# Attention scores in an encoder trunk: each head's high query rows over its low rows in one block of 128 rows, two products a head in place of three; order and places listed anew

## The chip, the cores and the metric

One Trainium2 chip, one of its cores. The metric is the device time of one execution in microseconds (us), the median of several runs. The core has five engines with a queue each: TensorE (PE, with PEld for its weight loads), VectorE (DVE), ScalarE (ACT), GpSimd (POOL) and SyncE (SP, which here issues DMA transfers). An engine works its queue off in order and waits where an instruction needs another engine's result.

## The reference

A trunk of two layers on an input `x` of 256 tokens by 1024 values, all in 32-bit floats. Each layer is a feed-forward block, a mixer and another feed-forward block, each followed by a layer norm. The mixer of layer 0 is a bidirectional mLSTM, that of layer 1 attention over a window of 128 tokens:

```python
for l in range(DEPTH):                       # 2
    x = layer_norm(ALPHA * x + 0.5 * swiglu(x, ffn_w_in[l, 0], ffn_w_out[l, 0]), ...)
    y = mlstm_mixer(x, ...) if l % 2 == 0 else window_attention(x, ...)
    x = layer_norm(ALPHA * x + y, ...)
    x = layer_norm(ALPHA * x + 0.5 * swiglu(x, ffn_w_in[l, 1], ffn_w_out[l, 1]), ...)
# window_attention: 16 query heads, 4 key/value heads, 64 values a head
p = x @ w_in                                 # q, k, v
s = q . k * HEAD_DIM ** -0.5 - slope * |t - s|        # masked where |t - s| > 128
m = max(max(s), sink);  pe = exp(s - m)
attn = pe / (sum(pe) + exp(sink - m))
y = (attn . v) @ w_out
```

## The kernel before

There are six stages, one behind the other: feed-forward, mLSTM, feed-forward, feed-forward, attention, feed-forward. Tokens are worked in two tiles of 128 (`t`).

**Precise products.** TensorE multiplies in a format that rounds its operands, so every operand is split in two: ACT copies it into the rounded format (`_hi`) and DVE subtracts that from the original (`_lo`). `mm3` then sums three products into one bank: hi by hi, hi by lo, lo by hi. Each weight piece of 128 x 1024 is loaded by DMA into a raw buffer (`w_raw`, `s_raw`), split into `w_hi` (ACT) and `w_lo` (DVE), and used by PE. The split buffers are a ring of ten. The feed-forward stages save products by a scheme with sums of weight blocks, some of them made by accumulating DMAs that POOL issues.

**Attention.** `proj` makes k, v and half of q; `k_turn` and `q_turn` transpose k and q on PE and split them into `kk` (hi, lo) and `q2`. k is written twice into the rows it is transposed from, so in `kk` rows 0 to 63 and rows 64 to 127 hold the same key head. `q_rest` makes the other half of q already transposed, in four parts spread over the first steps. A step `j` of eight handles two heads `a` = 0, 1. `scores(j)` multiplies, and one DVE instruction (in the profile CUSTOM_DVE_ANT_0 with a READ_ACCUMULATOR, in the order ISA) adds the distance term and leaves the row extreme in `nm`; ACT takes the exponential and sums it; POOL divides (`scale`); PE transposes (`turn`, products with `ident`), ACT and DVE split the result (`pr_hir`, `pr_lor`); `values` multiplies with v; ACT and DVE gather `o`, which is split into `q2`'s old place of that step; `out_proj` multiplies it with `at_w_out`. `q_rest` and `out_proj` are fitted in between. Before, the hi rows of both heads of a step stood in `q2[:, j, 0]` (head a on rows 64a to 64a + 63) and the lo rows in `q2[:, j, 1]`, and a product had 64 rows of contraction.

**What sets the order.** Nothing is issued as the Python code runs: `Program` records every operation, and `issue` plays them in the order that the table of numbers `ORDER` gives (differences of the recorded indices). `SLOTS` gives each tile's place in its ring, one character per use. So every instruction in the profile carries the line of `Engine`'s `issue` call (L317 before, L276 after), and has to be told by its tiles: `p` is a bank of TensorE's results, `q2r` is `q2`, `sc` the scores.

Of the kernel before, what the change touches and what calls it, by code (L numbers as in the profile page):

```python
# [39 lines left out]
    "0 10 -9 8 2 -9 11 -10 11 15 1 -26 11 1 -11 12 1 -12 13 12 -24 13 1 11 -10 1 1 1 1 1 8 -7 17 -37 28 10 1 72 "  # L40
    "-71 -15 104 -103 15 -10 134 -136 13 140 -139 -11 17 -5 100 -114 15 46 -58 17 -16 17 -16 1 17 24 117 -142 -6 "
    "19 -18 112 -105 131 -137 11 19 -12 1 4 -3 4 1 -4 5 -19 1 19 122 -140 13 -10 32 -34 48 -45 1 157 -156 13 36 "
    "-48 21 -6 47 -40 -6 148 -147 32 14 -40 1 42 -10 -38 1 10 -9 30 46 -45 6 1 9 -8 60 -67 8 -7 1 10 38 99 -140 "
    "-31 161 -71 -95 49 100 -93 -26 13 1 34 -72 199 -160 -27 32 -4 60 -59 26 -25 -41 -6 56 -46 1 1 38 -43 89 -39 "
    "-49 43 1 -43 97 -53 110 -105 39 -38 1 3 -44 52 -10 1 77 -41 66 -100 -51 86 -85 116 -52 30 -29 1 -15 -50 66 "
    "-63 48 107 -106 42 -41 72 -55 1 -66 62 18 1 -14 -4 19 47 -65 4 1 1 13 -30 18 19 57 -56 55 -49 1 1 4 45 -56 "
    "8 11 -7 1 -4 5 -13 19 52 -70 55 -19 20 147 -146 -44 -12 18 1 -18 58 -39 213 -212 69 -33 157 -178 26 77 -132 "
    "38 76 -84 141 -115 -50 9 4 86 -73 31 -32 26 -37 38 -19 15 -33 43 -29 30 1 -7 -107 119 -49 45 17 -16 -8 9 53 "
    "-99 47 -34 36 2 -13 -37 16 57 -3 -9 30 -82 40 -39 41 1 1 21 100 -110 -10 1 10 -9 36 -10 11 -22 132 -141 32 "
    "-81 86 122 -146 34 -14 91 -110 -10 11 -76 66 81 -52 14 -32 1 1 92 -75 -29 32 49 -48 -44 26 -11 12 45 -44 88 "  # L50
    "38 -125 -17 258 -240 97 -82 1 27 -67 57 17 -33 -16 26 -25 149 -133 10 1 -10 15 -4 -6 -4 15 9 -13 20 -6 -20 "
    "21 1 -11 52 -51 1 152 -100 1 70 -69 -44 50 -32 -17 40 -37 -26 46 45 -78 24 -23 13 1 -22 93 -70 45 -44 239 "
    "-222 -16 78 -66 24 33 -52 44 -17 58 -89 1 23 -53 54 216 -253 61 -17 34 55 -88 1 16 -15 16 109 -171 273 -268 "
    "3 243 -150 -95 57 27 130 -156 14 157 -167 -21 3 41 -40 1 1 16 -15 40 -15 -9 23 -45 23 16 8 1 37 -124 102 "
    "-27 13 -25 9 -32 49 14 178 -191 47 -61 189 -201 9 207 -185 -1 2 8 -25 26 1 1 -61 65 -14 1 -24 64 -30 -37 83 "
    "-55 1 -23 35 -3 -29 30 24 11 -31 41 -27 -15 12 4 -14 58 -47 -10 1 18 -34 73 -56 1 12 -11 7 9 20 -10 120 104 "
    "-238 7 161 -160 1 71 103 -173 21 -20 187 -173 -13 84 -81 -14 -68 83 -18 63 74 -92 -26 9 20 -19 17 -16 1 52 "
    "-63 51 -37 15 -14 -14 43 -42 -31 59 1 63 -78 1 -14 15 229 -228 113 -100 198 -210 13 12 147 -165 7 -13 190 "
    "-147 3 -15 -6 1 -12 13 -12 43 -30 1 3 168 -184 1 1 1 55 -41 16 -15 111 -86 -24 1 126 -102 70 -93 278 -265 "
    "-6 130 -109 -45 41 70 -69 98 -97 3 -14 12 48 153 -227 29 1 1 103 -125 23 -49 215 -161 -24 -3 113 -85 -23 28 "  # L60
    "1 -37 -6 38 6 90 -95 -24 30 1 -6 84 -77 1 1 1 1 -10 11 6 78 -77 1 92 -27 -64 3 1 -12 9 123 -119 71 -44 14 "
    "-44 33 99 -121 23 -22 78 -59 221 -220 -28 31 -22 -8 262 -261 117 -87 72 -94 3 1 21 94 -114 44 -43 44 -27 62 "
    "-34 -27 10 -8 26 69 -84 228 -258 46 1 -46 23 80 -100 -10 1 33 -26 18 34 -51 119 -52 -45 -20 21 7 -4 94 -34 "
# [1423 lines left out]
```

## Time and profile before

| what | value |
| --- | --- |
| median of 3 runs | 915.05 us (914.67 to 915.2) |
| the profiled execution: span from its first to its last instruction | 914.29 us |
| the profiled execution's own time | given by its span alone |
| instructions | 12376 |
| granted TensorE clock | 0.998 of full speed |
| DMA | 208.52 MB, mean 228 GB/s |
| attention stage | about 645 to 731 us |
| score products on PE | 670.0 to 709.9 us |

Of the rows that follow: `busy` is the time in which an engine worked on such an instruction; products overlap on PE, so their pace is read from the distance of their starts. `[0.68 <-ACT o L317]` behind a row is idle time of the engine ahead of it and what ended it. A row `670.83:711.44 ...` gives busy time with the count of instructions for PE, PEld, DVE, ACT and POOL in that stretch, then the granted clock, the DMA share and GB/s.

### The profile page before, as it was taken

To read this page: it belongs to the slowest core of one execution; us is meant where nothing else is said; L and a number is where in the kernel's file an instruction comes from. 1 tells how busy PE (TensorE), PEld (TensorE's weight loads), DVE (VectorE), ACT (ScalarE), POOL (GpSimd) and SP (SyncE) were. 2 spreads that over 40 slices of the span, in tenths; PEclk is the share of its full clock that TensorE was granted. 3 is DMA by queue.
4 is the path that set the end of the run, shared out by engine and by line. 5 is a ranking of instruction groups with operands and counts; after the bars stand their busy time and mean duration, and the time that the engine had idled before them with its cause. 6 is when DMAs were issued, how large, how long until landed. Compare 5 with 4: busy or idle time off the path is not lost.

```text
span 914.3 us, 12376 instructions
## 1 busy us (share of the span) xinstructions
PE 903.8 (99%) x4382; PEld 748.2 (82%) x4382; DVE 812.8 (89%) x987; ACT 576.8 (63%) x796; POOL 156.8 (17%) x200
## 2 busy tenths in 40 slices
PE   9999999999999999999999999999999999999996
PEld 7888888889988888887888888888887788888885
DVE  6998989997798999888999988899899899988897
ACT  6667567557655677565747666666488557666560
POOL 0211112113311121111012111120435311202110
PEclk9999999999999999999999999999999999999999
DMA  9999889558273889898957899987543396997971
GB/s 334 299 298 298 246 248 240 180 179 263 94 260 114 270 252 256 269 280 197 341 196 188 229 277 296 277 178 259 173 173 116 116 277 166 257 303 174 321 182 46
DMA packets 100670, 208.52 MB, mean 228 GB/s; under 512 B 6872, under 2 KB 21232, under 8 KB 100608
## 3 DMA queue, kind: packets, MB, share of 16 engines
q1 hardware_dynamic: 82832, 173.83, 54.1%
q0 software_dynamic: 17632, 33.64, 22.4%
q8 instruction: 34, 0.56, 0.2%
q10 hardware_dynamic: 144, 0.26, 0.1%
q14 instruction: 28, 0.23, 0.1%
HBM read 206.65 MB, written 1.05 MB: 227 GB/s over the span
## 4 chain that ended last, share of the span: by engine, by line
PE 96%; DMA 2%; DVE 1%; issue 1%; ACT 0%; DVEq 0%; POOL 0%; POOLq 0%
PE p L317 96%; DMA s_raw<-in_ffn_w_in_dram 1%; DMA ln_g<-in_ln_g_dram 1%; DVE w_lo L317 0%; DVE x L317 0%; ACT w_hi L317 0%; DVE h_lor L317 0%; DVEq L1483 0%; DVE hc_lor L317 0%; DVE t L317 0%; ACT xT_hi L317 0%; DVE stats L317 0%; DVE mv L317 0%; POOL ji L317 0%; DVE ident L317 0%
## 5 line engine op out<-in xcount | busy, mean ns | idle before, releaser
L317 ACT CAST w_hi<-s_raw 128x1024 fp32r<-128x1024 f32 x239 | 244.5, 1051 | 94.5 <-PE p L317 56.4
L317 DVE TENSOR_TENSOR w_lo<-s_raw,w_hi 128x1024 fp32r<-128x1024 f32 x239 | 285.6, 1218 | 19.6 <-ACT w_hi L317 15.6
L317 ACT CAST w_hi<-w_raw 128x1024 fp32r<-128x1024 f32 (+1 forms) x167 | 172.1, 1041 | 77.9 <-PE p L317 37.6
L317 DVE TENSOR_TENSOR w_lo<-w_raw,w_hi 128x1024 fp32r<-128x1024 f32 (+1 forms) x167 | 199.8, 1208 | 14.5 <-ACT w_hi L317 13.3
L317 PE MATMUL p<-w_hi,xT_hi 128*128 128x512 f32 x512 | 191.9, 394 | 0.8 <-ACT w_hi L317 0.5
L317 PE MATMUL p<-w_lo,xT_hi 128*128 128x512 f32 x512 | 192.1, 394 | 0.0
L317 PE MATMUL p<-w_hi,xT_lo 128*128 128x512 f32 x512 | 191.3, 394 | 0.0
L317 PE MATMUL p<-w_hi,h_lor 128*128 128x512 f32 (+1 forms) x323 | 119.9, 390 | 0.1
L317 PE MATMUL p<-w_hi,h_hir 128*128 128x512 f32 (+1 forms) x323 | 119.5, 391 | 0.0
L317 PE MATMUL p<-w_lo,h_hir 128*128 128x512 f32 (+1 forms) x323 | 118.6, 389 | 0.0
L317 PEld LDWEIGHTS p<-w_hi,xT_hi 128*128 128x128 f32 x512 | 95.8, 188 | 20.4 <-ACT w_hi L317 1.0
L317 PEld LDWEIGHTS p<-w_lo,xT_hi 128*128 128x128 f32 x512 | 96.0, 188 | 19.5 <-DVE w_lo L317 0.4
L317 PEld LDWEIGHTS p<-w_hi,xT_lo 128*128 128x128 f32 x512 | 96.1, 188 | 19.3 <-DVE xT_lo L317 0.3
L317 POOL DMA_DIRECT2D s_raw<-in_ffn_w_in_dram x43 | 52.2, 1266 | 329.0 <-DVE w_lo L317 90.5
L317 PE MATMUL p<-w_hi,S_hir 128*128 128x512 f32 x256 | 96.9, 390 | 0.0
L317 PE MATMUL p<-w_hi,S_lor 128*128 128x512 f32 x256 | 96.8, 390 | 0.0
L317 PE MATMUL p<-w_lo,S_hir 128*128 128x512 f32 x256 | 96.8, 390 | 0.0
L317 PEld LDWEIGHTS p<-w_hi,h_lor 128*128 128x128 f32 x323 | 60.6, 188 | 12.6 <-DVE h_lor L317 0.5
L317 PEld LDWEIGHTS p<-w_lo,h_hir 128*128 128x128 f32 x323 | 60.7, 188 | 12.2
L317 PEld LDWEIGHTS p<-w_hi,h_hir 128*128 128x128 f32 x323 | 60.5, 188 | 12.3 <-ACT h_hir L317 0.2
L317 PEld LDWEIGHTS p<-w_hi,S_hir 128*128 128x128 f32 x256 | 48.0, 188 | 10.5 <-ACT t L317 0.4
L317 PEld LDWEIGHTS p<-w_lo,S_hir 128*128 128x128 f32 x256 | 48.1, 188 | 10.1 <-DVE w_lo L317 0.2
(187 smaller groups left out, 1176.7 us busy)
## 6 DMA issues: line engine op xcount, KB each, us to landing
s_raw<-in_ffn_w_in_dram SPq DMA_DIRECT2D x101, 512.0 KB, 6.0
w_raw<-in_ffn_w_in_dram SPq DMA_DIRECT2D x58, 512.0 KB, 6.3
s_raw<-in_ffn_w_out_dram SPq DMA_DIRECT2D x55, 512.0 KB, 5.8
s_raw<-in_ffn_w_in_dram POOLq DMA_DIRECT2D x43, 512.0 KB, 7.1
w_raw<-in_ffn_w_out_dram SPq DMA_DIRECT2D x33, 512.0 KB, 7.1
w_raw<-in_ml_w_in_dram SPq DMA_DIRECT2D x24, 512.0 KB, 5.2
w_raw<-in_ffn_w_in_dram POOLq DMA_DIRECT2D x21, 512.0 KB, 7.8
s_raw<-in_ffn_w_in_dram SPq DMA_DIRECT2D x20, 256.0 KB, 6.1
```

What stands on the lines that cost most here:

```text
L317: f(*args, **kw)
```

## The change

Each head's 64 hi rows are put on partitions 0 to 63 and its 64 lo rows on 64 to 127 of one block `q2[:, j, a]`. Since both halves of `kk` hold the same keys, one product of 128 rows with `kk` hi gives q_hi k_hi + q_lo k_hi, and one with `kk` lo gives q_hi k_lo + q_lo k_lo. A head and token tile so takes two products of 128 rows instead of three of 64, and the sum has the lo by lo term besides. The evacuations of q into `q2` are done once for each head half, on 64 partitions each. ORDER and SLOTS are new lists from end to end.

```diff
 ORDER = (
-    "0 10 -9 8 2 -9 11 -10 11 15 1 -26 11 1 -11 12 1 -12 13 12 -24 13 1 11 -10 1 1 1 1 1 8 -7 17 -37 28 10 1 72 "
...
 SLOTS = {
-    "raw.0": ("210375894260ab315798a1b2380476593806142893750a61b4735a0286b12a940280"),
+    "raw.0": ("0143256891a2b0734568b203751469a87519234867ab051923a7b509812475630984"),
...
@@ q_turn
                 for j in range(4):
                     nc.tensor.transpose(p[:, j], qd[t][:, j], ident)
-                split_evac((q2[:, 0:4, 0, tok(t)], q2[:, 0:4, 1, tok(t)]), p)
+                for a in range(2):
+                    split_evac((q2[0:64, 0:4, a, tok(t)], q2[64:128, 0:4, a, tok(t)]), p[64 * a:64 * a + 64])
@@ q_rest
                         j = 4 + 2 * g + f
-                        split_evac((q2[:, j, 0], q2[:, j, 1]), p, qs_col[:, j - 4:j - 3])
+                        for a in range(2):
+                            r = slice(64 * a, 64 * a + 64)
+                            split_evac((q2[0:64, j, a], q2[64:128, j, a]), p[r], qs_col[r, j - 4:j - 3])
@@ scores
                 for t in range(2):
-                    for n_, (qe, ke) in enumerate(((0, 0), (0, 1), (1, 0))):
-                        for a in range(2):
-                            r = slice(64 * a, 64 * a + 64)
-                            nc.tensor.matmul(ps[a][:, t], q2[r, j, qe, tok(t)], kk[ke][r, g], start=n_ == 0, stop=n_ == 2)
+                    for a in range(2):
+                        for e in range(2):
+                            nc.tensor.matmul(ps[a][:, t], q2[:, j, a, tok(t)], kk[e][:, g], start=e == 0, stop=e == 1)
```

The numbers of instructions change by 32 products fewer on PE (64 score products for 96) and six split pairs more (six instructions each on ACT and DVE); the rest is the same work in another order.

PE at the scores of step 2. Before:

```order
L317 MATMUL p4_92<-xT_lo_137,w_hi8_76 128x256
L317 MATMUL p2_90<-kk_hir_4_0_227,q2r_4_0_238 128x256
L317 MATMUL p2_90<-kk_lor_4_0_228,q2r_4_0_238 128x256
L317 MATMUL p5_93<-kk_hir_4_0_227,q2r_4_0_238 128x256
L317 MATMUL p2_90<-kk_hir_4_0_227,q2r_4_0_238 128x256
L317 MATMUL p5_93<-kk_lor_4_0_228,q2r_4_0_238 128x256
L317 MATMUL p5_93<-kk_hir_4_0_227,q2r_4_0_238 128x256
L317 MATMUL p0_88<-ident_144,sc_4_5_234 128x128
```

The same place on PE after (`p5` and `p4` are the banks of heads 0 and 1):

```order
L276 MATMUL p3_91<-xT_hi_136,w_lo3_81 128x256
L276 MATMUL p6_94<-ident_144,sc_4_5_234 128x128
L276 MATMUL p5_93<-kk_hir_4_0_227,q2r_4_0_238 128x256
L276 MATMUL p5_93<-kk_lor_4_0_228,q2r_4_0_238 128x256
L276 MATMUL p4_92<-kk_hir_4_0_227,q2r_4_0_238 128x256
L276 MATMUL p4_92<-kk_lor_4_0_228,q2r_4_0_238 128x256
L276 MATMUL p6_94<-ident_144,sc_4_5_234 128x128
```

Six products of one token tile, the heads in turn, have become four, hi and lo keys in turn. In both programs the 16 groups stand in 18 unbroken runs.

DVE ahead of and in the first score step. Before:

```order
L317 TENSOR_TENSOR w_lo_78<-w_raw_67,w_hi_70 128x1024
L317 TENSOR_TENSOR kk_lor_0_228<-p_94,kk_hir_0_227 128x4x128
L317 TENSOR_TENSOR sc_1_230<-p_90,qs_row_0_225 128x512
L317 TENSOR_TENSOR w_lo_87<-w_raw_66,w_hi_72 128x1024
L317 ISA sc_5_234,nm_2_243<-p_89,dist_0_235,neg_sink 128x256
L317 ISA nm_2_243 128x1
L317 ISA sc_5_234,nm_2_243<-p_95,dist_0_235,neg_sink 128x256
L317 ISA nm_2_243 128x1
L317 TENSOR_TENSOR q2r_0_238<-p_90,q2r_0_238 128x4x128
L317 TENSOR_TENSOR w_lo_82<-w_raw_64,w_hi_69 128x1024
L317 ISA sc_1_230,nm_2_243<-p_89,dist_0_235,neg_sink 128x256
```

The same place on DVE after:

```order
L276 TENSOR_TENSOR sc_2_231<-p_95,qs_row_0_225 128x512
L276 TENSOR_TENSOR kk_lor_0_228<-p_91,kk_hir_0_227 128x4x128
L276 TENSOR_TENSOR w_lo_86<-w_raw_66,w_hi_77 128x1024
L276 TENSOR_TENSOR q2r_0_238<-p_94,q2r_0_238 64x4x128 x2
L276 ISA sc_4_233,nm_0_241<-p_93,dist_0_235,neg_sink 128x256
L276 ISA nm_0_241 128x1
L276 ISA sc_5_234,nm_0_241<-p_93,dist_0_235,neg_sink 128x256
L276 ISA nm_0_241 128x1
L276 ISA sc_5_234,nm_0_241<-p_92,dist_0_235,neg_sink 128x256
L276 ISA nm_0_241 128x1
L276 ISA sc_4_233,nm_0_241<-p_92,dist_0_235,neg_sink 128x256
```

The evacuation of the second half of q stands ahead of the first reduction and in two pieces, and no weight split is left between the reductions of step 0. From the first to the last reduction, before there are 32 reductions, 11 `pr_lor`, 8 `w_lo`, 8 `o`, 4 scaled `q2r` of 256 columns, 4 `q2r<-o`, one `q2r<-p` of 512 columns and one `v1r`; after, 32 reductions, 12 `pr_lor`, 5 `w_lo`, 10 `o`, 8 scaled `q2r` and 4 `q2r<-o`. On ACT the same stretch has 7 `w_hi`, 4 scaled `q2r` and 4 `q2r<-o` before, and 6, 6 and 5 after.

SP's queue at the program's start. Before:

```order
L317 DMA x_134<-in_x_dram 128x512
L317 DMA w_raw_66<-in_ffn_w_in_dram 128x512 x2
L317 DMA w_raw_65<-in_ffn_w_in_dram 128x2x512
L317 DMA x_134<-in_x_dram 128x512
L317 DMA w_raw_64<-in_ffn_w_in_dram 128x2x512
L317 DMA x_135<-in_x_dram 128x512
L317 DMA w_raw_67<-in_ffn_w_in_dram 128x2x512
```

SP's queue there after:

```order
L276 DMA x_134<-in_x_dram 128x512
L276 DMA w_raw_64<-in_ffn_w_in_dram 128x512 x2
L276 DMA w_raw_65<-in_ffn_w_in_dram 128x2x512
L276 DMA w_raw_66<-in_ffn_w_in_dram 128x2x512
L276 DMA w_raw_67<-in_ffn_w_in_dram 128x2x512
L276 DMA s_raw_0_102<-in_ffn_w_in_dram 128x2x512
L276 DMA x_135<-in_x_dram 128x512
L276 DMA x_134<-in_x_dram 128x512
```

The second halves of the two token tiles of `x` now follow three more weight loads. PE's first transpose of such a half stands behind 11 wide products (128 x 512) before and behind 24 after. On POOL the loads of the small tensors (`gw`, `gbias`, `gcol`, `sink`) stand ahead of the first accumulating weight load, where before they were spread over the first two stages and later.

More of the change, by code (lines that the diff above doesn't have):

```diff
@@ L39 @@
 ORDER = (
[208 rows of a table removed]
[188 rows of a table added]
 )
 SLOTS = {
-    "raw.0": ("210375894260ab315798a1b2380476593806142893750a61b4735a0286b12a940280"),
-    "p": ("3015273416371651624740737037743003470071732475045321703262751465120457615023462034756305172461503713"
-        "6442055504252022042555024574651034561742340220420324423044423643153426021762340152301647420765314722"
-        "060227602276670206205326743621306753342132312243113214236"),
-    "h_hir.0": ("01001"),
-    "h_lor.0": ("10101"),
-    "w_hi": ("1536089427819056375820935612483172106249564780132954061782549302675180974325916874210359678241306597"
-        "8240637195824063718459026378591430268719546372150862437689061249085367241903758623104975268413908217"
-        "5469870321659748031256784901375628147093568273041695371208346897520134659782013465920871649356809217"
-        "5368049215063874921506387491206537891234706592318672398160257386541934670253891457260389415762058963"
-        "905268715496"),
@@ L261 @@
-    "w_lo": ("8138121742486951046580796125370164658235182350986541234970895268317504678250734095386210549378012564"
-        "3185206793418250671824930568271469351690561739512805381576130867846245869374921053769842501271093864"
-        "2053149782160345781269073541976208452176048318292137523486914603568274168732498103528769175083257419"
-        "2653801479153869204715368940125739846550169834160253046821795345869732804613859740863742798750286574"
-        "365018925167"),
-    "t.0": ("10423251205145435305135232350"),
@@ L295 @@
-    "t.5": ("22311504210332350204153145144"),
+    "raw.0": ("0143256891a2b0734568b203751469a87519234867ab051923a7b509812475630984"),
+    "p": ("0123547602431650271634161463143634361631465302147630525174630127436012472356014361750423506107346521"
+        "7064603063046030603430463502107342561702420302304203020343042350614273064517236045172653046237510434"
+        "266364232346263426326437517043526107535747547357475743473"),
+    "w_hi": ("0143256890147325689014732568901473256890147325689014732568901473256890147325689014732568901732456890"
+        "1732456890173245689017324568901732456890173245689017324568901732456890173245689017324568901732456890"
+        "1732456890173245689017324568901732456890173245689017324568901732456890173245689017324568901732456890"
+        "1732456890173245689071345628907134562890713456289071345628907134562890713456289071345628907134562890"
+        "713456289071"),
@@ new lines @@
+    "w_lo": ("0143256789014325678901432567890143256789014325678901432567890143256789014325678901432567890143256789"
+        "0143256789014325678901432567890143256789014325678901432567890143256789014325678901432567890143256789"
+        "0143256789014325678901432567890143256789014325678901432567890143256789014325678901432567890143256789"
+        "0143256789014325678901425637890142563789014256378901425637890142563789014256378901425637890142563789"
+        "014256378901"),
+    "t.0": ("02453140250321543210432501345"),
@@ new lines @@
+    "raw.1": ("13012301230123012301230123012301"),
+    "wt.1": ("3210"),
+    "a_lor.1": ("1010"),
+    "raw.2": ("9546782306179548a2b39758426ab013426078a3b419526078149250367a42b8503a6719b85039ab671850426b78109543a2"
+        "1093b85241a67093b8a1607329b510487325"),
+    "t.2": ("4123450214135042350123541032403150241303524015243152034513"),
+    "sc.4": ("3145025402135402135402"),
+    "raw.4": ("43254325432514032541"),
+    "raw.5": ("02103324591a678b03246a7b839025148395ab0428167395ab18637549a0832b7540"),
@@ L296 @@
+    "t.5": ("03121540312354103542035124301"),
 }
```

27 lines of the change are left out of this document (removed), and 395 rows, old and new, of the table ORDER.

## The prediction

> **What bounds the kernel now.** I read the page first, then the chain of waits, then who waits for whom on TensorE.
>
> ```profile
> PE 903.8 (99%) x4382; PEld 748.2 (82%) x4382; DVE 812.8 (89%) x987; ACT 576.8 (63%) x796; POOL 156.8 (17%) x200
> PE 96%; DMA 2%; DVE 1%; issue 1%; ACT 0%; DVEq 0%; POOL 0%; POOLq 0%
> PE p L317 <- DVE t L317: 0.3, 1, 0.3
> ```
>
> The first line is busy time per engine, the second the share of the chain that ended last, the third the whole list of PE's waits between 20 and 906 us. TensorE issues its products one behind the other for 886 us and waits 0.3 us in all. So time is won only by fewer or cheaper PE slots, and lost where a new order lets PE wait. DVE, at 89%, is the next engine; what it is asked for in one stage can pass what PE takes there.
>
> The products of the change stand between 670 and 710 us, in the attention stage. This is PE around one group of six old score products:
>
> ```profile
> 677.02 0.28 PE L317 MATMUL p<-xT_lo,w_hi 128*128 128x256 f32 x1
> 677.23 0.39 PE L317 MATMUL p<-kk_hir,q2r 64*128 64x256 f32 x2
> 677.45 0.28 PE L317 MATMUL p<-kk_lor,q2r 64*128 64x256 f32 x2
> 677.57 0.28 PE L317 MATMUL p<-kk_hir,q2r 64*128 64x256 f32 x2
> 677.78 0.39 PE L317 MATMUL p<-xT_hi,w_hi 128*128 128x256 f32 x1
> 678.00 0.28 PE L317 MATMUL p<-xT_hi,w_lo 128*128 128x256 f32 x1
> 678.12 0.29 PE L317 MATMUL p<-xT_lo,w_hi 128*128 128x256 f32 x1
> ```
>
> Columns: start, length, what, count. Lengths overlap, so I read the distance of the starts. Two products of full height (128 rows by 256 columns) start 0.12 us apart (678.00 to 678.12). The step into 64 rows takes 0.21 (677.02 to 677.23), the first pair 0.22, a pair in the middle 0.12, the last pair with the step back 0.21, and the first full product behind it 0.22. From 677.02 to 678.00 are 0.98 us; two full products would take 0.24, so the six cost 0.74: three pairs of 0.12, and 0.38 that lies at the steps in and out.
>
> **PE's part of the change.** Before, 96 products of 64 rows: 48 pairs. In the order they stand in 18 unbroken runs (16 groups, some torn by another operation). 48 x 0.12 + 18 x 0.38 = 12.6 us. After, 64 products of 128 rows and 256 columns, by the row of the same size 64 x 0.12 = 7.7 us, with no change of height. PE gains 4.9 us. The lower end counts only sixteen whole groups: 16 x (0.74 - 0.48) = 4.2. The upper end adds the waits of weight loads in this stretch for the row maxima `nm`, which may go with shorter groups:
>
> ```profile
> PEld p L317 <- DVE nm L317: 1.3, 4, 0.4
> ```
>
> 4.9 + 1.3 = 6.2. I take 4.9, since the row above is a whole undisturbed group and the runs are counted.
>
> Trainium skill, "TensorEngine Tiling (Array Packing)": its tiling table gives up to twice the speed for contractions of at most 64 rows, because two row tiles work at once, and its key properties say that changing the tiling mode drains the engine. The pair at 0.12 agrees with the first, and the 0.38 at the steps with the second. By the first rule alone a group would be 0.36 before and 0.48 after, and PE would lose 16 x 0.12 = 1.9 us.
>
> **DVE's part.** The stretch from the first to the last score reduction on DVE, 670.83 to 711.44 us:
>
> ```profile
> 670.83:711.44 40.61, 40.61 (x281) 31.76 (x279) 37.26 (x101) 35.34 (x99) 24.91 (x51) 1.00 0.30 95
> L317 DVE CUSTOM_DVE_ANT_0 sc<-p,dist,neg_sink 128x256 f32<-128x256 f32 x32 | 14.3, 479 | 1.6 <-PE p L317 1.1 <-issue 0.3
> L317 DVE TENSOR_TENSOR pr_lor<-p,pr_hir 128x512 fp32r<-128x512 f32 x11 | 7.6, 687 | 1.0 <-ACT pr_hir L317 1.0
> L317 DVE TENSOR_TENSOR w_lo<-w_raw,w_hi 128x1024 fp32r<-128x1024 f32 x6 | 7.3, 1218 | 0.0
> L317 DVE TENSOR_TENSOR w_lo<-s_raw,w_hi 128x1024 fp32r<-128x1024 f32 x2 | 2.4, 1219 | 0.0
> L317 DVE TENSOR_TENSOR o<-p,o 64x256 f32<-64x256 f32 x8 | 3.4, 422 | 0.9 <-ACT o L317 0.7
> L317 DVE SCALAR_TENSOR_TENSOR q2r<-p,qs_col,q2r 128x256 fp32r<-128x256 f32 x4 | 1.8, 480 | 0.2 <-ACT q2r L317 0.2
> L317 DVE TENSOR_TENSOR q2r<-o,q2r 128x256 fp32r<-128x256 f32 x4 | 1.7, 418 | 0.0
> L317 DVE TENSOR_TENSOR q2r<-p,q2r 128x512 fp32r<-128x512 f32 x1 | 0.7, 691 | 0.1
> L317 DVE TENSOR_TENSOR v1r<-p,v1r 128x256 fp32r<-128x256 f32 x1 | 0.4, 418 | 0.0
> ```
>
> The first row gives busy time of PE, PEld, DVE (37.26), ACT (35.34) and POOL in 40.61 us; the others are DVE's work in it (count, busy, mean ns, idle ahead and for whom). DVE has 3.35 us to spare here. The new places of the two q halves need every evacuation of q twice, on 64 partitions each. Half the partitions save nothing: `o` on 64 x 256 takes 422 ns, `q2r` on 128 x 256 418. So the change costs four more scaled evacuations (4 x 480 ns) and two more of 512 columns (2 x 691) on DVE, 3.3 us in all.
>
> The new list of the order puts other work between the first and the last reduction: five weight splits `w_lo` instead of eight, eight scaled evacuations instead of four, twelve `pr_lor` instead of eleven, ten `o` instead of eight, and neither the `q2r<-p` nor the `v1r`. In us: -3 x 1.22 + 4 x 0.48 + 0.69 + 2 x 0.42 - 0.69 - 0.42 = -1.31. DVE then has 37.26 - 1.31 = 35.95 us of work here. PE's stretch would be 40.61 - 4.9 = 35.7 long. **So DVE, not PE, sets the length of this stretch.** Of its 3.35 us idle, the row of the reductions names 1.4 (1.1 for PE, 0.3 for nothing that shows); I let this go. Of the remaining 1.95, mostly waits for ACT, I let a third stay (0.65), as an engine that is late finds its inputs ready. 35.95 + 0.65 = 36.6: the stretch shrinks by 4.0 us. Ends: no idle time left -4.7; all of it left (39.3) -1.3.
>
> ACT gets twin copies too, and loses one split in the stretch (rows for 655 to 711 us, of which I use the means):
>
> ```profile
> L317 ACT CAST w_hi<-w_raw 128x1024 fp32r<-128x1024 f32 x11 | 11.4, 1048 | 1.3 <-ACT w_hi L317 0.8 <-PE p L317 0.5
> L317 ACT ACTIVATE q2r<-p,qs_col 128x256 fp32r<-128x256 f32 x4 | 1.8, 462 | 0.0
> L317 ACT CAST q2r<-o 128x256 fp32r<-128x256 f32 x4 | 1.6, 400 | 0.4 <-DVE o L317 0.4
> ```
>
> By the order six scaled copies instead of four, one `q2r<-o` more, one `w_hi` less: +0.92 + 0.40 - 1.05 = +0.3, so 35.6 of the new 36.6. ACT stays just below DVE. POOL (24.9) has the same scalings.
>
> **What is moved out of the stretch.** The three splits, `v1r` and three `q2r<-p` halves now stand ahead of the first reduction: 3.7 + 0.4 + 2.1 = 6.1 us more for DVE there. I cost this at nothing; the cover is idle time of DVE before it:
>
> ```profile
> 440.00:660.00 220.00, 220.00 (x1010) 181.11 (x1009) 199.21 (x214) 135.46 (x163) 34.37 (x45) 1.00 0.81 239
> 654.88 0.69 DVE L317 TENSOR_TENSOR xT_lo<-p,xT_hi 128x512 fp32r<-128x512 f32 x1 [1.90 <-ACT xT_hi L317]
> 656.86 0.69 DVE L317 TENSOR_TENSOR sc<-p,qs_row 128x512 f32<-128x512 f32 x1 [1.28 <-PE p L317]
> ```
>
> Between 440 and 660 DVE idles 20.8 us, and 3.2 us just ahead of the stage. If only these 3.2 could be used, the first scores would come 6.1 - 3.2 = 2.9 late, and after them `nm`, the exponentials on ACT and the turns on PE; that end goes into the range.
>
> **The rest of the order.** The same instructions are listed anew from end to end, about 870 us of them outside this stage. PE's work there is the same, and I cost the order at nothing. It can lose where transfers are short:
>
> ```profile
> 20.00:40.00 20.00, 20.00 (x94) 16.59 (x93) 19.20 (x21) 14.64 (x19) 2.72 (x3) 1.00 1.02 312
> 2.66 0.47 SPq L317 DMA_DIRECT2D x<-in_x_dram  x1
> DMA to landing us min/median/max: 3.3/5.0/6.6
> 10.14 0.27 PE L317 MATMUL p<-ident,x 128*128 128x128 f32 x1
> 563.13 0.39 PE L317 MATMUL p<-w_lo,xT_hi 128*128 128x512 f32 x1
> 565.40 0.39 PE L317 MATMUL p<-w_hi,xT_lo 128*128 128x512 f32 x1
> L317 POOL DMA_DIRECT2D gw<-in_ml_w_in_dram x1: 1421/1421/1421, 150.5 to 150.5; - x1
> 25.17 1.36 POOL L317 DMA_DIRECT2D w_raw<-in_ffn_w_in_dram  x1 [23.77 <-DMA s_raw<-in_ffn_w_in_dram]
> ```
>
> The DMA share is 1.02 at 312 GB/s there (the last two columns of the first row). On SP's queue the second halves of `x` now stand behind three more loads; a load of 0.52 MB takes 0.52/312 = 1.7 us, so they land up to 5.0 us later. PE turns the first of them behind 24 wide products instead of 11. Ten wide products take 2.27 us (563.13 to 565.40), so this covers 13 x 0.227 = 3.0. The half issued at 2.66 lands after about the median of 5.0, at 7.7, and is used at 10.14: 2.4 to spare. 3.0 + 2.4 is more than 5.0, so I cost it at nothing; without the spare time it is 2.0. POOL now issues `gw` and the other small loads first; its first accumulating load has 23.77 us of idle ahead of it, which hides the 1.4 us of `gw` and its like.
>
> **The sum.** The profiled execution spans 914.29 us; 914.3 - 4.0 = 910.3. The median of the runs, 915.05, is 0.76 above that span; with this, 911.05. About 0.2% (1.8 us) is what a measurement of this kernel can tell from no change.
>
> **Rivals.** (B) DVE gets by, because splits overlap better or PE's buffers take up its lag, and PE's own gain comes through whole: -4.9 to -6.2, 908.9 to 910.2. For it speaks that PE has waited for almost nothing anywhere; against it DVE's 37.26 of 40.61. (C) The stretch holds its length: the waits of DVE and ACT for each other (1.95 us) stay and new ones replace those for PE. -1.3, 913.8; no change that can be told. (D) Slower, at the start: with the DMA at 1.02, a load listed too late delays PE by 1.7 us each, and nothing gives it back. It decides from 5.8 us on (the 4.0 gained and the 1.8 of the bound), four loads uncovered: 4 x 1.7 = 6.8, 917.8. Against it: the list still has the loads in the order of use, and I find 2.0 us uncovered at the worst. (E) The steps of 0.38 do not belong to the height of 64 rows and remain; then sixteen groups cost 0.12 more each, PE +1.9 us, 917.0. Against it: full-height products of 256 columns follow each other at 0.12 in the row above. The tiling page's speedup rule, named above, is this rival.
>
> **How the numbers follow.** My forecast (DVE sets a stretch of 36 to 38 us) 0.53; B 0.19; C 0.14; D 0.06; E 0.04; small losses spread over the new order that leave it within 0.2%, 0.04. Faster 0.53 + 0.19 = 0.72, same 0.14 + 0.04 = 0.18, slower 0.10. The range goes from just below B (908.3) to C with 1.2 us more from a late start of the scores or of `x` (915.0); it holds the forecast, B and C, 0.86.
>
> **What would show it.** Right: 64 score products with starts 0.12 us apart and no step ahead of them; the stretch between first and last reduction about 36.6 us long with DVE above 97% busy; PE's waits there now on DVE (`nm`, `pr_lor`, `q2r`), 1 to 2 us in all. Wrong: DVE below 93% in the stretch (then C or a chain through ACT), PE waits of more than 1 us outside the attention stage, above all before 80 us (D), or groups of four products that take over 0.6 us (E).

## The result, and the profile after

The changed kernel takes 920.18 us (median of 4 runs, 919.6 to 921.6) against 914.86 of the kernel before beside it: ratio 1.0058 with an interval of 1.0044 to 1.0072. It is 5.3 us slower; the forecast was 4 us faster. Of the three views shown of before, the same of after. Busy time and the chain that ended last:

```profile
PE 902.2 (98%) x4350; PEld 750.7 (82%) x4350; DVE 812.0 (88%) x993; ACT 579.9 (63%) x802; POOL 158.6 (17%) x200
PE 58%; DMA 16%; DVE 15%; issue 5%; ACT 2%; POOL 2%; DVEq 0%; SPq 0%; POOLq 0%; ACTq 0%
```

The four longest entries of TensorE's waits between 20 and 906 us (in all, times, longest):

```profile
PE p L276 <- POOL sc L276: 1.7, 2, 0.9
PE p L276 <- DVE nm L276: 1.0, 2, 0.7
PE p L276 <- ACT h_hir L276: 1.0, 1, 1.0
PE p L276 <- ACT pr_hir L276: 0.6, 1, 0.6
```

PE's waits there, 0.3 us in all before, are 5.7 us after; these four entries are 4.3 of it. (PE's share of the chain fell from 96 to 58%, but the chain is no measure of lost time: much of what it gives to DVE and DMA lies behind 740 us, where PE lost only some 1.7 us.) The products themselves are what the change meant them to be. PE's products in time, around eight of the new score products:

```profile
678.52 0.28 PE L276 MATMUL p<-xT_hi,w_lo 128*128 128x256 f32 x1
678.64 0.28 PE L276 MATMUL p<-kk_hir,q2r 128*128 128x256 f32 x1
678.76 0.28 PE L276 MATMUL p<-kk_lor,q2r 128*128 128x256 f32 x1
...
679.48 0.28 PE L276 MATMUL p<-kk_lor,q2r 128*128 128x256 f32 x1
679.60 0.28 PE L276 MATMUL p<-xT_hi,w_hi 128*128 128x256 f32 x1
```

From 678.52 to 679.60 are nine distances of 0.12, with no step at either side: four products take 0.48, where six of 64 rows took 0.74.

Where the time went can be read from the starts of all PE products. With each at its unhindered distance (0.227 us for 512 columns, 0.119 for 256, 0.107 for 128), what PE loses besides is 5.2 us before and 8.2 after up to 20 us, 5.0 and 4.4 from there to 660, 8.9 and 9.5 from 660 to 740, 0.6 and 1.7 behind that. The 64 new products count 7.6 us by this measure and the 96 old ones 5.7 (two at once, without their steps), so the attention stage is 0.6 + 1.9 = 2.5 us longer. Of the 8.9 us lost there before, some 6 to 8 are the steps of the 64-row products. After, the steps are gone, and the 9.5 us lie at waits (3.8 us of them in the list for 660 to 740 us) and at the starts right behind them. Start +3.0, middle -0.6, attention +2.5, rest +1.1 make 6.0; the end behind the last product is 0.4 shorter, and the spans differ by 5.6.

Three places stand out. First the stretch from the first to the last score reduction in the attention stage (busy time of PE, PEld, DVE, ACT, POOL, then clock, DMA share, GB/s):

```profile
675.82:716.88 41.06, 38.38 (x244) 32.76 (x243) 36.67 (x104) 36.21 (x101) 24.11 (x45) 1.00 0.18 52
```

It is 41.06 us long, before 40.61. DVE's work in it fell from 37.26 to 36.67 us, but DVE and ACT each stand idle for 4 to 5 us. Second the way to it, here DVE's last pieces of q and its first score reduction:

```profile
674.38 1.41 DVE L276 TENSOR_TENSOR q2r<-p,q2r 64x512 fp32r<-64x512 f32 x2
675.82 0.48 DVE L276 CUSTOM_DVE_ANT_0 sc<-p,dist,neg_sink 128x256 f32<-128x256 f32 x1
```

The first reduction starts at 675.82 us, before at 670.83: 5.0 us later, while PE is only 2.4 behind at 660 us by the sums above. Third the start, here ACT's instructions and PE's longest wait:

```profile
5.03 0.62 ACT L276 CAST w_hi<-w_raw 128x512 fp32r<-128x512 f32 x1 [2.52 <-DMA w_raw<-in_ffn_w_in_dram]
9.97 0.62 ACT L276 CAST w_hi<-w_raw 128x512 fp32r<-128x512 f32 x1 [3.03 <-DMA w_raw<-in_ffn_w_in_dram]
10.63 0.98 PE L276 MATMUL p<-w_hi,xT_hi 128*128 128x512 f32 x2 [2.19 <-ACT w_hi L276]
```

ACT waits 3.03 us for a weight load, and PE 2.19 us for ACT.

### The profile page after: what moved, and what is told of

Same layout as the page of the kernel before. It is cut to its first block, busy times and chain, and to the rows that moved or that the text cites. A ratio compares the mean times of both kernels' runs of the same rounds, so it can differ in the third digit from the quotient of the medians.

```text
span 919.9 us, 12450 instructions
## 1 busy us (share of the span) xinstructions
PE 902.2 (98%) x4350; PEld 750.7 (82%) x4350; DVE 812.0 (88%) x993; ACT 579.9 (63%) x802; POOL 158.6 (17%) x200
## 4 chain that ended last, share of the span: by engine, by line
PE 58%; DMA 16%; DVE 15%; issue 5%; ACT 2%; POOL 2%; DVEq 0%; SPq 0%; POOLq 0%; ACTq 0%
PE p L276 58%; DVE w_lo L276 9%; DMA s_raw<-in_ffn_w_in_dram 9%; DMA w_raw<-in_ffn_w_in_dram 5%; DMA x<-in_x_dram 2%; DMA w_raw<-in_ml_w_in_dram 1%; DVE s_raw L276 1%; POOL sc L276 1%; ACT w_hi L276 1%; DVE t L276 1%; DVE w_raw L276 1%; POOL sm L276 1%; DVE x L276 1%; DVE h_lor L276 0%; DVE o L276 0%
## 5 line engine op out<-in xcount | busy, mean ns | idle before, releaser
L276 DVE TENSOR_TENSOR w_lo<-s_raw,w_hi 128x1024 fp32r<-128x1024 f32 x248 | 296.2, 1220 | 32.4 <-ACT w_hi L276 31.4
L276 ACT CAST w_hi<-s_raw 128x1024 fp32r<-128x1024 f32 x248 | 253.2, 1051 | 98.6 <-DVE s_raw L276 42.7
L276 DVE TENSOR_TENSOR w_lo<-w_raw,w_hi 128x1024 fp32r<-128x1024 f32 (+1 forms) x158 | 188.5, 1207 | 22.9 <-ACT w_hi L276 22.3
L276 PE MATMUL p<-w_hi,xT_hi 128*128 128x512 f32 x512 | 204.1, 399 | 2.4 <-ACT w_hi L276 2.2
L276 ACT CAST w_hi<-w_raw 128x1024 fp32r<-128x1024 f32 (+1 forms) x158 | 161.2, 1040 | 64.2 <-DVE w_raw L276 22.0
L276 PE MATMUL p<-w_hi,xT_lo 128*128 128x512 f32 x512 | 199.5, 391 | 0.0
L276 PE MATMUL p<-w_lo,xT_hi 128*128 128x512 f32 x512 | 199.5, 390 | 0.0
L276 PE MATMUL p<-w_hi,h_hir 128*128 128x512 f32 (+1 forms) x323 | 126.2, 391 | 1.0 <-ACT h_hir L276 1.0
L276 PE MATMUL p<-w_lo,h_hir 128*128 128x512 f32 (+1 forms) x323 | 125.1, 387 | 0.0
L276 PEld LDWEIGHTS p<-w_hi,S_lor 128*128 128x128 f32 x256 | 48.0, 188 | 10.0
```

Source lines behind the costliest of these rows:

```text
L276: f(*args, **kw)
```

## The experiments

All ratios are to the kernel before, run beside them on the same chip; 0.1% is 0.92 us. Stretch is from the start of the first to the start of the last score reduction in the profiled execution, by which the kernel before has 40.1 us with DVE 36.8 and ACT 34.9 busy, and the changed one 40.6 with 36.2 and 35.7.

| run | ratio, interval | stretch, DVE, ACT (us) |
| --- | --- | --- |
| e_oldlist | 1.0033, 1.0021 to 1.0046 | 43.0, 39.9, 38.1 |
| e_newlist | 1.0024, 1.0015 to 1.0033 | 38.8, 34.0, 33.6 |
| e_prodonly | 0.9987, 0.9978 to 0.9995 | 39.1, 36.6, 35.1 |
| e_twinonly | 1.0052, 1.0039 to 1.0064 | 43.9, 39.8, 38.1 |
| e_newprod | 1.0019, 1.0010 to 1.0028 | 38.4, 34.1, 33.5 |
| e_smalllate | 1.0033, 1.0021 to 1.0046 | as the changed kernel |
| e_xearly | 1.0055, 1.0043 to 1.0068 | as the changed kernel |
| e_lessdve | 0.9996, 0.9987 to 1.0005 | 40.0, 33.4, 34.8 |
| e_both | 0.9991, 0.9982 to 1.0000 | 38.3, 33.4, 34.7 |
| e_extrabehind | 1.0011, 1.0003 to 1.0020 | 41.1, 38.9, 36.8 |
| e_extraahead | 1.0017, 1.0008 to 1.0026 | 41.3, 38.9, 36.2 |
| e_wlopool | 1.0041, 1.0027 to 1.0055 | 43.6, 37.2, 38.4 |
| e_qpool | 1.0065, 1.0053 to 1.0078 | 45.2, 37.2, 35.7 |
| e_interleave | 1.0065, 1.0051 to 1.0079 | 45.1, 40.0, 38.3 |
| e_best | 1.0070, 1.0058 to 1.0083 | 42.7, 36.6, 35.7 |
| e_qsbuf | 1.0042, 1.0028 to 1.0056 | 43.9, 39.3, 39.3 |
| e_actless | 1.0037, 1.0024 to 1.0051 | 42.5, 39.7, 34.8 |
| e_dveless | 1.0025, 1.0016 to 1.0035 | 42.5, 36.5, 37.8 |

### The change taken apart: list, products, copies

Products and copies in the old list (the operations of the changed kernel, each at the place of the one it replaces), and the old operations in the new list:

```diff
 e_oldlist: operations of the changed kernel; ORDER and SLOTS of before, mapped
 e_newlist: operations of before; ORDER and SLOTS of the changed kernel, mapped
```

> The two full-height products a head and the twin copies of q, in the order and the places of the kernel before: each group of six old products is replaced by its four at the places of the last four of the six, each copy of q by its two halves one behind the other. In the changed kernel the 64 products took 0.12 us each where nothing held them (7.7 us against 11.8 for the old 96), but TensorE then waited some 5 us in the attention stage. Theory 1 (the products gain, the new list loses): PE gains 4.1 us here, less what the six more copies on DVE cost; 911 to 912.5, PE waits in the attention stage below 1.5 us. Rival (the chain of the scores through DVE, ACT and POOL sets the stage in any order): stretch from the first to the last reduction again 40 to 41 us, total 914 to 916.

> The three products of 64 rows a head and the single copies of q, as before, in the order and the places of the changed kernel (each group of six at the place where the second of a pair of the four stands). Theory 1 (products gain, list loses): everything outside the attention stage as in the changed kernel (+3.3 us against before), and the products 4.1 us dearer than in the changed kernel as far as its waits of 5 us do not take them up: 921 to 924. Rival (chain of the scores sets the stage): the same as the changed kernel, 920 within 0.7; the products make no difference.

Both theories fell. In the old list the change costs 3.0 us, and the new list with the old products costs 2.2: 3.1 of the 5.3 come with the products and copies whatever the order. So these two were taken apart, in the old list the products alone and the cut copies alone, in the new list the products alone:

```diff
 e_prodonly, e_newprod (q copied whole, as before)
-for n_, (qe, ke) in enumerate(((0, 0), (0, 1), (1, 0))): ...   # 3 products of 64 rows
+for a in range(2):
+    for e in range(2):
+        nc.tensor.matmul(ps[a][:, t], q2[:, j, e, tok(t)], kk[e][:, g], ...)
 e_twinonly (old products)
-split_evac((q2[:, j, 0], q2[:, j, 1]), p, qs_col[:, j - 4:j - 3])
+for a in range(2):
+    r = slice(64 * a, 64 * a + 64)
+    split_evac((q2[r, j, 0], q2[r, j, 1]), p[r], qs_col[r, j - 4:j - 3])
```

> The kernel before with its order and places, q copied as before (one copy of full height), and only the score products changed: two of 128 rows a head, which take q's block of high rows of both heads and then that of low rows. Left out by this: the cross terms of the split, the scores are other numbers; every other operation is as before. PE's work in the stage falls by 4.1 us, DVE's and ACT's stay. Theory P (PE set the stage before, and only the six extra copies on DVE make DVE set it): 3.5 to 4.2 us faster than before. Theory D (DVE with its 3 to 4 us of waits for ACT and PE set the stretch before too): 0 to 1 us faster, and PE waits 3 us or more in the stage, mostly on DVE. Theory T (both are tied): 1 to 3 faster.

> The kernel before with its order, places and its three products of 64 rows, but each copy of q cut into two pieces of 64 partitions, to the old places: six more instructions on ACT and six on DVE (3.3 us of DVE), nothing else. With new products and these copies in the old order the time was 3.1 us above before. Theory D or T: the stretch between first and last reduction grows by 2.5 to 3.3 us, 2.5 to 3.5 slower than before. Theory P: DVE's 3.35 us of idle time in the stretch takes most of it, less than 1.5 slower.

> The changed kernel's order and places, with its two products a head, but q copied once at full height as before (left out: the cross terms of the split, as in the run with the products alone in the old order). With the old products this list took 918.1 where before is 916.0, with new products and twin copies 5.3 above before. Theory T (PE, DVE and ACT are tied; the copies cost, the products give little): 0.5 to 2 us faster than with the old products, 916 to 917.5, so the copies cost 4 us or more in the new list too. Theory P (in the new list the products give their 4.1): 914. Rival (the copies do not matter in a list made for them): 920 to 921.5.

In the old list the products gain 1.2 us, the cut copies cost 4.8, both together 3.0 (the sum would be 3.6). In the new list the products gain 0.5 (1.0024 to 1.0019) and the copies cost 3.6 (1.0019 to 1.0058). The 0.5 lies within the intervals of its two runs. The copies are the larger part in either order. Theory P and the rival of the last run are out. Theory T fits the small gain of the products, but the copies cost more in the old list (4.8) and less in the new one (3.6) than it said.

### The start

```diff
 e_smalllate: changed kernel, ORDER only
-POOL: gw, gbias, gcol, sink loaded in the first 7 us
+POOL: the same loads behind the PE operation that they stand behind in the kernel before
 e_xearly: changed kernel, ORDER only
-SP: x, w, w, w, w, w, s_raw, x, x, s_raw, ...
+SP: x, w, w, w, x, w, w, x, s_raw, s_raw, ...
```

> The changed kernel with its small loads (gate weights gw, gbias, gcol, sink) and the scalings on POOL that belong to them moved from the first 7 us to the places where the kernel before has them. At the start PE lost 3.2 us more than before, of which 2.4 in one wait at 10.6 us for w_hi, whose load landed at 9.97 instead of before 7.3. Theory S (the small loads on POOL's queue hold up the wide ones): the wait at 10.6 us falls below 1 us, 917 to 918. Rival X (it is the place of the second halves of x and of three more weight loads on SP): no change, 920.

> The changed kernel with the loads of the two second halves of x moved up on SP, the one of the first row tile ahead of the fifth load of weights, the other ahead of the load behind that. Theory X (place of the loads on SP's queue): the start loses 1 us or more less, 917.5 to 919. Rival S (the small loads on POOL's queue): no change at the wait for w_hi at 10.6 us, 919.5 to 920.5; the short waits for x at 15 to 16 us (0.7 us in all) may go.

With the small loads late the cost is 1.0033 against 1.0058, 2.3 us less; the earlier loads of x give nothing in all. The stretch from 4 to 7 us, first of the changed kernel (columns as above), then with the small loads late, then with x early:

```profile
4.00:7.00 3.00, 2.88 (x16) 2.67 (x16) 1.32 (x3) 1.73 (x3) 2.63 (x6) 1.00 0.85 224
```

```profile
4.00:7.00 3.00, 3.00 (x13) 2.71 (x13) 1.29 (x2) 1.14 (x3) 0.00 (x0) 1.00 0.87 298
```

```profile
4.00:7.00 3.00, 2.95 (x16) 2.48 (x16) 1.29 (x2) 1.64 (x3) 2.63 (x6) 1.00 0.99 305
```

ACT's load in the run with the small loads late, then ACT's load and PE's longest wait behind it in the run with x early:

```profile
8.25 0.62 ACT L257 CAST w_hi<-w_raw 128x512 fp32r<-128x512 f32 x1 [0.67 <-DMA w_raw<-in_ffn_w_in_dram]
```

```profile
8.31 0.62 ACT L256 CAST w_hi<-w_raw 128x512 fp32r<-128x512 f32 x1 [1.22 <-DMA w_raw<-in_ffn_w_in_dram]
16.80 0.51 PE L256 MATMUL p<-w_hi,xT_hi 128*128 128x512 f32 x1 [1.39 <-ACT xT_hi L256]
```

The wait of 3.03 us for the load falls in both runs, to 0.67 and to 1.22. With the small loads late the time comes back; with x early PE waits 1.39 us at 16.80 instead, for ACT's copy of the turned x. So the early small loads cost 2.3 us, but how they do it stays open: a loss of DMA throughput alone it isn't, since the run with x early has the same small loads on POOL and moves 305 GB/s.

### What the stage is bound by

```diff
 e_lessdve: before;  e_both: e_prodonly;  e_dveless: e_oldlist
-nc.vector.tensor_add(o[top], p[low, 0], o[top])
-nc.vector.tensor_add(o[low], p[top, 1], o[low])
 e_actless: e_oldlist
-nc.scalar.copy(o[top], p[top, 0]); nc.scalar.copy(o[low], p[low, 1]); (and the two additions)
+nc.vector.tensor_copy(o[top], p[top, 0]); nc.vector.tensor_copy(o[low], p[low, 1])
 e_wlopool: e_oldlist, three of the stage's splits
-nc.vector.tensor_sub(lo, raw, hi.bitcast(F32))
+nc.gpsimd.tensor_sub(lo, raw, hi.bitcast(F32))
```

> The kernel before with its order and places, without the sixteen additions to o on DVE behind the products of the values (0.42 us each, 6.7 us in the stage; the low part of the split is left out of the attention's output). Theory D: the stretch shrinks by about 3 us, 2.5 to 3.5 faster than before. Theories P and T: PE, which waited for nothing there, still needs its time: within 0.5 of before.

> The kernel before with its order and places and two reliefs at once, which alone gave 1.2 (products of full height, PE 4.1 us less) and 0.4 us (without the additions to o, DVE 6.7 us less); left out are the cross terms of the split and the low part of the attention's output. Theory T (PE and DVE tied, each stays when the other is relieved): 3 to 4.5 us faster than before. Rival (a chain through ACT and POOL, exponentials and scalings, sets the stage): 1 to 2 faster, the sum of the two.

> New products and twin copies in the order and places of before (919.2 there against 916.0 of before), and three of the eight weight splits w_lo that stand in the stretch on POOL instead of DVE. DVE is relieved of 3.7 us, a little more than the twin copies brought. Theory D or T: at least the 3.1 us come back, 915.5 to 916; if PE's 4.1 us then come through whole (theory P), 912. Rival: POOL, in order, holds up the scalings of the scores behind the splits, and DVE's time goes into waits for it: 919 or more.

> New products and twin copies in the order and places of before (3.1 us above before), with ACT relieved: the sixteen copies to o (0.36 us each, some ten of them in the stretch of the score reductions) stand on DVE in place of its sixteen additions, so DVE has the same number of instructions; the low part of the attention's output is left out. In nine of the kernels run so far, between the first and the last reduction, the length was ACT's busy time and 3.6 to 5.8 us, whatever PE and DVE had. Theory A (ACT's queue, with its five us of waits, sets the stretch): the stretch falls from 43.0 to 39 to 40.5 us, 2 to 3.5 us faster than with ACT's copies, at or just above before. Rival (DVE, or all three): less than 1 us faster.

> The same kernel with DVE relieved instead: the sixteen additions to o are left out (0.42 us each, some ten in the stretch, as in the run on before that gained 0.4), ACT keeps its copies. Theory A (ACT's queue sets the stretch): less than 1 us faster than with them, the stretch stays above 42. Rival (DVE's queue sets it): 2.5 to 4 us faster, the stretch at 39 to 40.5. If both relieve by about the same, neither engine alone sets it but the chain through both.

Before, DVE's relief is worth nothing that can be told, PE's 1.2 us, and both together no more (0.8): not a tie of PE and DVE, and theory T falls with it. With the cut copies, three splits fewer on DVE leave the time; ten copies fewer on ACT leave it; ten additions fewer on DVE give at most 0.8 us, within the intervals. Theory A, that ACT's queue sets the stretch, fell too (42.5 where 39 to 40.5 were expected). TensorE's waits for DVE's copies of q from 650 to 760 us, of the run with copies and products in the old list, then with DVE relieved:

```profile
PE p L295 <- DVE q2r L295: 3.8, 5, 1.2
```

```profile
PE p L295 <- DVE q2r L295: 3.9, 5, 1.2
```

The same five waits stand in both, and with ACT relieved too (3.8 us in five): neither relief touches them. In the kernel before there are none.

### Number or place of the copies

Extra instructions in the kernel before, as many and as large as the cut copies add, but reading SBUF and read by nobody, behind or ahead of each copy of q:

```diff
 e_extrabehind (e_extraahead: ahead of it)
 split_evac((q2[:, j, 0], q2[:, j, 1]), p, qs_col[:, j - 4:j - 3])
+nc.scalar.activation(dm[0][r, 0], dist[r, 0], AF.Copy, scale=scale)
+nc.vector.scalar_tensor_tensor(dm[1][r, 0], dist[r, 0], scale, dist[r, 1], ...)
```

> The kernel before, all its operations, order and places as they were, and behind each of the six copies of q one more instruction on ACT and one on DVE, of the size of a half copy (64 partitions, 512 columns twice, 256 columns four times), from SBUF into a tile that nobody reads. Cutting the copies in two in this order cost 4.4 to 4.8 us. Theory E (what counts is that ACT's and DVE's queues, in order, get 2.9 and 3.2 us more to do): 3.5 to 5 slower than before. Theory B (a bank of PSUM and the data are held longer by the second piece): here the copy itself ends as before, less than 1.5 slower.

> The same extra instructions, but listed ahead of each copy on ACT and on DVE, so that the copy ends later by one instruction of each engine, and the bank of PSUM is held longer. Theory E: as with the extra ones behind, within 0.7. Theory B: 3.5 to 5 slower, and at least 2.5 more than with the extra ones behind.

They cost 1.0 and 1.6 us where the cut copies cost 4.8, although DVE is nearly as busy (38.9 us, with the cut copies 39.8) and then for 94 to 95% of the stretch. Theory E falls: most of the cost is not the engines' time. Theory B falls as it was put, since the intervals of the runs "ahead" and "behind" overlap. In the run "ahead" ACT's extra instruction stands straight ahead of the four scaled copies and holds each up by 0.4 us (extra at 678.48, copy at 678.88); ahead of the second unscaled one it runs in idle time and holds nothing up (extra at 669.07, copy at 670.65). That is a shorter hold than the pieces' own, seen next.

What the pieces do is seen in the old list. ACT's two high pieces, then DVE's two low ones (x2 each), and below them the two whole copies of the kernel before:

```profile
672.04 1.18 ACT L295 CAST q2r<-p 64x512 fp32r<-64x512 f32 x2 [2.10 <-PE p L295]
673.24 1.41 DVE L295 TENSOR_TENSOR q2r<-p,q2r 64x512 fp32r<-64x512 f32 x2 [0.53 <-ACT q2r L295]
```

```profile
671.20 0.59 ACT L317 CAST q2r<-p 128x512 fp32r<-128x512 f32 x1 [1.63 <-PE p L317]
671.82 0.69 DVE L317 TENSOR_TENSOR q2r<-p,q2r 128x512 fp32r<-128x512 f32 x1
```

DVE begins when both high pieces have ended, and stands idle for 0.53. From 672.04 to 674.65 are 2.61 us; the kernel before needed 1.31 (671.20 to 672.51). Where scaled pieces stand, the same bank is next used by a product, and PE waits for the last of four on DVE (PE, then DVE):

```profile
689.17 0.39 PE L295 MATMUL p<-kk_hir,q2r 128*128 128x256 f32 x1 [0.81 <-DVE q2r L295]
687.13 1.98 DVE L295 SCALAR_TENSOR_TENSOR q2r<-p,qs_col,q2r 64x256 fp32r<-64x256 f32 x4
```

Three tries to take this away, in the old list (the third also in the new one, with the small loads late):

```diff
 e_qpool:      ACT copies the scaled p whole to SBUF; POOL makes the four pieces from there
 e_qsbuf:      ACT copies the scaled p whole to SBUF; ACT and DVE make the four pieces from there
 e_interleave, e_best (ORDER only)
-ACT hi 0, ACT hi 1, ..., DVE lo 0, DVE lo 1
+ACT hi 0, DVE lo 0, ACT hi 1, ..., DVE lo 1
```

> New products in the order and places of before, but the four scaled twin copies of q are taken apart: ACT writes the scaled product once, full height, to SBUF (0.46 us, after which the PSUM bank is free), and POOL makes the two high and two low pieces from there, in its idle time ahead of the next row sums. The second head's block holds the low rows above, which changes no sum. In the run with twin copies in this order PE waited 3.8 us for the copies of q, three times because the next product or turn uses the bank that a scaled copy still reads (1.39, 0.97, 0.83 us) and twice for the unscaled copies ahead of the first scores (0.96, 0.47). Theory B (the twin copies cost by holding a bank and by ACT's and DVE's time): the three waits go, the two stay, 915.5 to 916.5 on the scale where before is 916.0 and the twin copies 919.2. Rival (POOL's scalings come late behind the pieces, chain of the scores): PE waits for sc of POOL instead, 918.5 or more.

> The kernel with new products and twin copies in the order and places of before (3.1 us above before), with one thing changed: the first low piece on DVE is listed between the two high pieces on ACT. With both high pieces listed first, the first low piece began only when the second high piece had ended (672.62 to 673.19 on ACT, DVE from 673.22), because its one wait covers both; now each low piece has its own wait. Every instruction and the order on ACT are the same; DVE's first piece moves up by a few places. Theory B (the pieces cost because they stand in series between q's product and what waits for its bank or its data): a copy's chain is 0.47 to 0.58 us shorter six times, PE's 3.8 us of waits for copies of q fall to 2.5 or less, 1 to 2 us faster than without, 1.2 to 2.2 above before. Rival (number of instructions): no change, 2.7 to 3.5 above before.

> The changed kernel, whole, with two things in its list moved: the small loads back to the places where before has them (alone: 2 us of the 5.3 came back), and for three of the four copies of q whose two high pieces stand together the first low piece between them. If both causes hold and add up: 2.2 to 3.2 us above before. If the pieces' wait does not matter in the new list: 3.1 above, as with the small loads alone.

> New products and twin copies in the order and places of before (3.1 us above before), but each of the four scaled products of q is first copied whole by ACT to SBUF (0.46 us), and the two high pieces on ACT and two low pieces on DVE read that copy. ACT has four instructions more than with twin copies (1.9 us), DVE the same number. PSUM's bank is read by one instruction instead of four in series (0.95 us on ACT, 0.97 on DVE). In the run without this PE waited three times, 3.2 us in all, for the next use of a bank that such pieces still read. Theory B (the pieces' series on the bank costs): these three waits fall to 0.6 us or less in all, 1 to 2.5 us faster than with the pieces from PSUM, 0.6 to 2.1 above before. Theory E (engine time): ACT's 1.9 us more make it 0.3 to 1.5 slower, 3.4 to 4.6 above before.

All expected gains failed, in three ways. (In the profiled executions of `e_qpool` and `e_best` about 1.7 us are a fall of the clock, told at the end.) With POOL's pieces PE waits 3.1 us for the scores that POOL scales behind them, as the rival had it:

```profile
PE p L295 <- POOL sc L295: 3.1, 2, 1.8
```

Interleaved, ACT's second high piece waits for DVE's first low piece, though they read different partitions of the bank (ACT, a scaled copy; and the sum of ACT's waits of that kind from 665 to 722 us):

```profile
681.50 0.47 ACT L295 ACTIVATE q2r<-p,qs_col 64x256 fp32r<-64x256 f32 x1 [0.61 <-DVE q2r L295]
```

```profile
ACT q2r L295 <- DVE q2r L295: 3.1, 5, 0.8
```

ACT's waits of that kind, none without the interleaving, are 3.1 us, and the run is 3 us slower than without. ACT and DVE here take the pieces of one bank strictly in the list's order. From SBUF they do not (the run `e_qsbuf`, ACT's two high pieces, then DVE's two low ones):

```profile
679.85 0.83 ACT L295 CAST q2r<-qs 64x256 fp32r<-64x256 f32 x2
680.29 1.00 DVE L295 TENSOR_TENSOR q2r<-qs,q2r 64x256 fp32r<-64x256 f32 x2 [0.47 <-ACT q2r L295]
```

DVE begins at 680.29 while ACT's second piece runs until 680.68, so it is the bank that keeps the pieces apart, not the tile `q2` that they write. The Trainium skill, "PSUM — Partial Sum Buffer", section "PSUM bank collisions raise a hardware error", says that two engines must not touch the same bank and the same 32 partitions at once, and that software guards it, in the simple version by the bank. The rows agree with a guard by the bank; that one by partitions would let the pieces overlap was not tried.

From SBUF all three of PE's bank waits (1.23, 0.81 and 0.67 us in the old list, at 682.73, 689.17 and 696.10) go, as theory B had it, and the time stays the same within its interval. The two waits for q that are left are those for the unscaled copies, and PE now waits for the row extremes:

```profile
PE p L295 <- DVE nm L295: 3.4, 3, 1.7
PE p L295 <- DVE q2r L295: 1.1, 2, 0.8
```

The bank alone is thus not the cause either. What is shown is this: the cut copies cost 3.6 us in the new list and 4.8 in the old; as many instructions that hang on nothing cost 1.0 to 1.6 in the old one; whichever wait of the copies was taken away, another of like size came in its place. That the rest comes from instructions that hang on q's product and stand in in-order queues ahead of the scores' own steps fits all of it, but no run shows it by itself. Which link of the loop DVE, ACT, POOL, PE would have to be shortened is left open.

## Why the prediction was wrong, step by step

- **PE's part: right in size, but little of it became time.** Groups of four take 0.48 us where nothing holds them, and no step is left. Sixteen whole old groups at 0.74 us are 11.8 us, the 64 new products 7.7, a gain of 4.2 (forecast 4.9, ends 4.2 and 6.2); by the starts of all 18 runs, torn groups and small waits included, the old products took 13.7. In the runs the products gained 1.2 us in the old list and 0.5 in the new. Rival E, that the steps stay, is out.
- **DVE's and ACT's work in the stretch: nearly right.** Forecast 35.95 and 35.6 us, measured 36.7 and 36.2.
- **"I let a third stay (0.65)": the step that failed.** The idle time of DVE was to fall from 3.35 to 0.65 us; it rose to 4.4. The stretch came out at 41.06 instead of 36.6, 4.5 us of the 9.6 by which forecast and measured span differ. It was taken for granted that an engine asked for 36 of 36.6 us finds its inputs ready; over all the runs DVE idled for 2.1 to 8.1 us of the stretch and ACT for 3.6 us or more, whichever engine was relieved. Rival C (waits of DVE and ACT for each other stay, new ones replace those for PE) had the mechanism, but only as "no change"; it left out that the cut copies make new waits.
- **The cut copies priced by count: failed.** 3.3 us on DVE were set against DVE's room. They cost 3.6 in the new list and 4.8 in the old, where instructions of the same count and size that hang on nothing cost 1.0 to 1.6.
- **"What is moved out of the stretch", costed at nothing: failed as well, near the end it named (2.9).** PE is 2.4 us behind at 660 us, but DVE's first reduction starts 5.0 us late: 2.6 us more. With the small loads late PE is not behind at 660 us, and the reduction still starts 2.5 us late (673.33):

```profile
673.33 0.48 DVE L257 CUSTOM_DVE_ANT_0 sc<-p,dist,neg_sink 128x256 f32<-128x256 f32 x1
```

  The new list with the old operations shows the same: it takes 2.8 us of DVE's work out of the stretch (36.8 to 34.0), the stretch is 1.3 us shorter, and it starts 2.4 us later than PE's lag of 1.6 at 660 us explains. What the list moved out was paid ahead of the stretch.
- **The start: right place, wrong cause.** The wait came before 80 us, as the test for rival D had it, worth 2.3 us, not 6.8. I had looked at the places of x on SP, which in all change nothing, and let POOL's first load of 23.77 us of idle time cover `gw`. It covers POOL's time; that the early small loads hold up something else was not priced. With PE's 2.4 us at 660, the 2.6 ahead of the stretch and the 4.5 in it, 9.5 of the 9.6 us are placed.
- **"The rest of the order" at nothing: right on the whole.** With the start taken out, the new list costs 2.2 - 2.3 = -0.1 us, though no run has both the old operations and the small loads late.

## What to carry to other kernels

An operation is not priced by its count where queues are in order: ask what its input waits for, what stands behind it in its queue, and who next needs the bank it reads. A stretch in which two or three engines hand work round at about 90% each did not shrink in step with the busiest engine's work here; keep its measured idle time in the sum, or add to it, and price when the stretch begins as well as how long it is. Do not price a small load by its issuing engine's idle time alone: look at the waits for the large loads beside it.

## What was not expected of the hardware

In the profiled executions of two runs the granted clock fell to about half behind a long wait of PE (1.80 and 1.81 us of idle time shown): first e_qpool, the product behind the wait, then the four us after it by two (columns as above, the clock third from the end); then the same of e_best.

```profile
699.38 0.33 PE L295 MATMUL p<-ident,sc 128*128 128x128 f32 x1 [1.80 <-POOL sc L295]
```

```profile
700.00:702.00 2.00, 1.88 (x7) 1.40 (x7) 1.22 (x1) 0.00 (x0) 2.00 (x4) 0.55 0.00 0
702.00:704.00 2.00, 2.00 (x10) 1.69 (x8) 0.95 (x3) 1.99 (x7) 1.79 (x6) 0.59 0.57 138
```

```profile
687.27 0.50 PE L256 MATMUL p<-pr_hir,v0r 128*128 128x512 f32 x1 [1.81 <-ACT pr_hir L256]
```

```profile
688.00:690.00 2.00, 2.00 (x8) 1.70 (x8) 1.34 (x5) 1.23 (x6) 0.00 (x0) 0.50 0.00 0
690.00:692.00 2.00, 1.74 (x8) 1.24 (x6) 0.55 (x3) 0.35 (x2) 1.75 (x3) 0.68 0.00 0
```

Four us at 0.57 cost about 1.7 us, as much as the wait, and this is in the spans of these two executions. A wait hardly shorter, 1.70 us in `e_qsbuf`, left the clock at 1.00:

```profile
690.46 0.39 PE L295 MATMUL p<-kk_hir,q2r 128*128 128x256 f32 x1 [1.70 <-DVE nm L295]
```

```profile
690.00:692.00 2.00, 1.54 (x12) 1.50 (x13) 1.77 (x7) 1.16 (x4) 1.24 (x5) 1.00 0.00 0
```

The Trainium skill, "TensorE: Matmul & The Clock Gate", section "What's actually happening", puts the fall to half speed behind an idle window of about 3.4 us; here a wait of 1.8 us was enough, while the wait of 2.19 us at 10.6 us of the changed kernel did not do it (1.00 from 10 to 12 us). So the length of the wait alone does not decide it, and what else does is not shown.
